# Decoder layer: rotated part of the latent attention's scores in one matmul of full floats in place of three passes of split operands

## The chip, the cores and the metric

One core of one Trainium2 chip. The metric is the device time of one execution in microseconds, median of several runs; lower is better. A core has TensorE (matmuls, weight loads beside them), VectorE (DVE), ScalarE (ACT), GpSimd (POOL) and SyncE (SP), each with its own queue, and DMA engines.

## What is computed

One decoder layer over 512 tokens of width 2048: modulation, a combined input projection, two attentions (A with a sparse selection of keys, B with latent keys and values), gates, an output projection and a convolutional feed-forward part. The change concerns attention B: 8 heads, whose queries and keys have 128 plain dimensions and 64 rotated ones.

```python
mq = (rms_norm(mq_lat, g_mq_lat) @ w_mq_up).reshape(B, S, M_HEADS, M_NOPE + M_ROPE)
mkv = (rms_norm(mkv_lat, g_mkv_lat) @ w_mkv_up).reshape(B, S, M_HEADS, M_NOPE + M_V)
...
mk = rms_norm(jnp.concatenate([mk_nope, mk_r], axis=-1), g_km)
mq = rms_norm(mq, g_qm)
mq = jnp.concatenate([mq[..., :M_NOPE], apply_rope(mq[..., M_NOPE:], *rope_m)], axis=-1)
mk = jnp.concatenate([mk[..., :M_NOPE], apply_rope(mk[..., M_NOPE:], *rope_m)], axis=-1)
...
logits = jnp.einsum('bthd,bshd->bhts', q_b, k, preferred_element_type=jnp.float32) * scale
logits = jnp.where(causal[None, None], logits, -jnp.inf)
p = jax.nn.softmax(logits, axis=-1).astype(v.dtype)
return jnp.einsum('bhts,bshd->bthd', p, v).reshape(B, Q_BLOCK, H * dv)
```

The scores of a head are thus a sum of a product over 128 dimensions and one over 64.

## The kernel before, in words

Activations and weights lie in SBUF in tiles of 128 rows and 512 columns ("slots", 81 of them, handed out by `get` and given back by `put`). Results of matmuls go to eight banks of PSUM. Two kinds of matmul are used. The projections split each operand into a high part of type float32r and a low part, the rest (`split`: a copy on ScalarE, line 138, and a subtraction on VectorE, line 139; `wtile` does the same for weights, lines 130 and 131) and run three passes: high by high, high by low, low by high (lines 142 to 144). Some products in the attentions run as one matmul of plain float32; in the trace such a matmul is two records.

Work goes in stages: modulation and input projection; attention A with gates; the remaining gates by a scheme of seven products (line 1072 on); then attention B with the projection of A's output; the projection of B's output (`w_pb`); the output projection (`w_o`); the feed-forward part.

In the attention B stage, `up_pair(hp)` projects queries, keys and values of two heads from the latents (`lin_tm`), normalizes and rotates them in `ev_up` and `ev_qup`, and transposes them (lines 1165, 1169, 1200, 1204) so that the dimension lies on the rows. The plain parts get a tile per head (`kT[a]`, `qT[a]`); the rotated parts of both heads share one, head `a` in rows 64a to 64a+63, which is split (lines 1170 and 1205) into `kTr` and `qTr`. `attend_pair(hp)` then takes both heads through `attend`: for each of four blocks of 128 queries, the longest first, the scores `qk` go into a bank, with S = 512, 384, 256, 128 keys. A score block is four matmuls:

```python
W = max(S, 256)
PE.matmul(o[:, :W], qh[rs, qs], kh[rs, :W], start=True, stop=False)
PE.matmul(o[:, :W], qh[rs, qs], kl[rs, :W], start=False, stop=False)
PE.matmul(o[:, :S], qT[a][:, qs], kT[a][:, :S], start=False, stop=False)
PE.matmul(o[:, :W], ql[rs, qs], kh[rs, :W], start=False, stop=True)
```

Three of them (lines 1219, 1220, 1222) have 64 rows, since `rs` is half of the rows; the third (line 1221) has 128 rows and plain floats. Behind a block comes the softmax on VectorE and ScalarE (lines 689 to 692), behind four blocks the transposes of the probabilities (line 700) and the product with the values (line 708, plain floats), whose result is split (lines 710 and 711) and, but for the last two heads, stored to DRAM.

`pa_block` (the projection of A's output, three passes) stands between the pairs of heads, and a background stream multiplies modulation weights on VectorE (line 747). The order on each engine isn't that of the source: a scheduler orders instructions by priorities and its own estimate of times, so score blocks stand between matmuls of projections. Weight loads of SP go ahead at high priority (`wtile`), as buffers come free.

Of the kernel before, what the change touches and what calls it, by code (L numbers as in the profile page):

```python
# [14 lines left out]
AF = mybir.ActivationFunctionType  # L15
# [16 lines left out]
def trunk_layer_kernel(  # L32
# [21 lines left out]
    V, A, G, PE, SP = nc.vector, nc.scalar, nc.gpsimd, nc.tensor, nc.sync  # L54
# [14 lines left out]
    def get(dt=F32):  # L69

        i = min(free, key=lambda n: rested[n])
        free.remove(i)
        if cur[i] is None or cur[i].dtype != dt:
            cur[i] = pool.tile([P, T], dt, name=f"slot{i}", tag=f"slot{i}")
        held[id(cur[i])] = i
        return cur[i]

    def getr():
        return get(F32R)

    def put(*ts, lag=2):

        for t in ts:
            i = held.pop(id(t))
            rested[i] = clock[0] + lag
            free.append(i)
# [26 lines left out]
    def r32(ap):  # L113
        return ap.bitcast(F32)
# [22 lines left out]
    def split(dst_hi, dst_lo, src):  # L137
        A.activation(dst_hi, src, AF.Copy)  # L138
        V.tensor_tensor(dst_lo, src, r32(dst_hi), ALU.subtract)  # L139
# [103 lines left out]
    def rsqrt_mean(dst, ss, n, w):  # L243
        v = sm.tile([P, w], F32, name="rsm")
        V.tensor_scalar(v, ss, 1.0 / n, EPS, op0=ALU.mult, op1=ALU.add)
        G.tensor_tensor(dst, v, mhalf[:, :w], ALU.pow)
# [271 lines left out]
    def at_bank():  # L518
        cnt["at"] += 1
        return AT[cnt["at"] % 4]  # L520
# [6 lines left out]
    b = bank[7]  # L527
# [10 lines left out]
    b = bank[6]  # L538
# [7 lines left out]
    for tb in range(1, 4):  # L546
        S = (tb + 1) * P
        qiT = []
        for cb in range(2):
            t = qi[tb, cb]  # L550
            rope(t.rearrange("p (h d) -> p h d", d=64), 8, 16, "i", tb)
            b = at_bank()
            for q in range(4):
                PE.transpose(b[:, q * P:(q + 1) * P], t[:, q * P:(q + 1) * P], ident)
            o = (getr(), getr())
# [5 lines left out]
        for hd in range(16):  # L561
            ps = slice((hd % 2) * 64, (hd % 2) * 64 + 64)
            q = (hd % 8) // 2
            b = at_bank()
# [40 lines left out]
    def head_ss(dst, src3, i):  # L605
        n, d = src3.shape[1], src3.shape[2]
        t = sq[i % 2][:, :n * d].rearrange("p (n d) -> p n d", n=n)
        A.activation(t, src3, AF.Square)
        V.tensor_reduce(dst, t, axis=AX.X, op=ALU.add)
# [16 lines left out]
    for g in range(2):  # L626
        b = at_bank()
# [46 lines left out]
    def attend(*a):  # L674
        attend_pv(*attend_p(*a))
# [251 lines left out]
    def operands(act, ts):  # L927
        return (quarter(act, 0, 0), quarter(act, KH, 0), quarter(act, KH, HT)) + tuple(sums(ts, n) for n in range(4))
# [14 lines left out]
    def seven(work, pairs_of_banks, hook=None, AHEAD=2):  # L943
        def pair_steps(n, p):
            bx, by = pairs_of_banks[n % len(pairs_of_banks)]
            X, Y, Z = bx[:, :HT], by[:, :HT], by[:, HT:]
            L, E = {}, {}
            W = p.K * P
            g1, g2 = p.scale or (None, None)
# [5 lines left out]
            def load(blk):  # L955
                t = rawq.popleft()
                SP.dma_start(t[:, :W], p.load(blk))
                return t

            def hilo(t):  # L960
                i = cnt["wt"] % len(hi_b)
                cnt["wt"] += 1
                hi, lo = hi_b[i][:, :W], lo_b[i][:, :W]
                split(hi, lo, t[:, :W])
                return hi, lo

            def comb(o, a, b, op):
                V.tensor_tensor(o[:, :W], a[:, :W], b[:, :W], op)  # L968

# [116 lines left out]
    for i in range(KH // 2):  # L1086
        raw = [get() for _ in range(4)]
        ta, tb_ = get(), get()
        for j in range(2):
            k, o = 2 * i + j, slice(j * HT, (j + 1) * HT)  # L1090
# [10 lines left out]
    def gate_out(i):  # L1101
        def fin(u1, u2):
            G.dma_start(gate_d[G0 + 2 * i], u1)
            G.dma_start(gate_d[G0 + 2 * i + 1], u2)
            put(u1, u2)
        return fin
# [10 lines left out]
    def gate_hook(q, n):  # L1117
        gate_tick()
        if q == n - 7:
            reload_mq()  # L1120

    rs = operands(h, h_sums)
    start, run = seven([Pair(rs, lambda blk, i=i: w_gs[i, blk], gate_out(i)) for i in range((31 - G0) // 2)],
          ((MM[0], MM[1]), (MM[2], MM[3])), gate_hook)
# [10 lines left out]
    def up_pair(hp):  # L1135
        kn = [get() for _ in range(2)]
        vv = [get() for _ in range(2)]
        kr = get()
        kr3 = kr.rearrange("p (t a d) -> p t a d", t=4, a=2)

        def two(ts, tb):
            o = (tb % 2) * 256
            return ts[tb // 2][:, o:o + 256].rearrange("p (n d) -> p n d", n=2)

        def ev_up(tb, b, kn=kn, vv=vv, kr3=kr3, two=two):
            b4 = b.rearrange("p (n e d) -> p n e d", n=2, e=2)
            k3 = two(kn, tb)
            A.activation(k3, b4[:, :, 0, :], AF.Copy)
            V.tensor_copy(two(vv, tb), b4[:, :, 1, :])
            ss = sm.tile([P, 2], F32, name="ss2")  # L1150
            head_ss(ss, k3, tb)
            V.tensor_scalar(ss, ss, ss_kr[:, tb:tb + 1], None, op0=ALU.add)
            r = sm.tile([P, 2], F32, name="rs2")
            rsqrt_mean(r, ss, 192, 2)
            V.tensor_tensor(k3, k3, r[:, :, None].to_broadcast([P, 2, P]), ALU.mult)
            for a in range(2):
                V.tensor_scalar(kr3[:, tb, a], krot[:, tb], r[:, a:a + 1], None, op0=ALU.mult)

        lin_tm(w_mkv_up, hp * 512, 512, kvT, 2, MM, ev_up)
        kT = [get(), get()]  # L1160
        kTr = (getr(), getr())
        for a in range(2):
            b = at_bank()
            for tb in range(4):
                PE.transpose(b[:, tb * P:(tb + 1) * P], two(kn, tb)[:, a, :], ident)
            A.activation(kT[a], b, AF.Copy, scale=gkm_col)
        b = at_bank()
        for tb in range(4):
            PE.transpose(b[:, tb * P:(tb + 1) * P], kr[:, tb * P:(tb + 1) * P], ident)
        split(*kTr, b)  # L1170
        put(*kn)
        put(kr)

        qn = [get() for _ in range(2)]
        qr = get()
        qr3 = qr.rearrange("p (t a d) -> p t a d", t=4, a=2)
        nsc_b = sm.tile([P, 4, 2], F32, name="nsc_b", bufs=3)

        def ev_qup(tb, b, qn=qn, qr3=qr3, nsc_b=nsc_b, two=two):
            b3 = b.rearrange("p (n d) -> p n d", n=2)  # L1180
            q3 = two(qn, tb)
            A.activation(q3, b3[:, :, 0:P], AF.Copy)
            V.tensor_copy(qr3[:, tb], b3[:, :, P:192])
            ss = sm.tile([P, 2], F32, name="ss2")
            t = sq[tb % 2][:, :384].rearrange("p (n d) -> p n d", n=2)
            A.activation(t[:, :, 0:P], q3, AF.Square)
            A.activation(t[:, :, P:192], qr3[:, tb], AF.Square)
            V.tensor_reduce(ss, t, axis=AX.X, op=ALU.add)
            r = sm.tile([P, 2], F32, name="rs2")
            rsqrt_mean(r, ss, 192, 2)  # L1190
            V.tensor_scalar(nsc_b[:, tb], r, -(192 ** -0.5), None, op0=ALU.mult)
            rope(qr3[:, tb], 2, 64, "qm", tb)

        lin_tm(w_mq_up, hp * 384, 384, mqT, 4, MM, ev_qup)
        qT = [get(), get()]
        qTr = (getr(), getr())
        for a in range(2):
            b = at_bank()
            for tb in range(4):
                PE.transpose(b[:, tb * P:(tb + 1) * P], two(qn, tb)[:, a, :], ident)  # L1200
            A.activation(qT[a], b, AF.Copy, scale=gqm_col)
        b = at_bank()
        for tb in range(4):
            PE.transpose(b[:, tb * P:(tb + 1) * P], qr[:, tb * P:(tb + 1) * P], ident)
        split(*qTr, b)
        put(*qn)
        put(qr)
        pairs[hp] = (qT, qTr, kT, kTr, vv, nsc_b, two)

    def attend_pair(hp):  # L1210
        qT, qTr, kT, kTr, vv, nsc_b, two = pairs.pop(hp)
        for a in range(2):
            rs = slice(a * 64, (a + 1) * 64)

            def qk(o, qb, S, a=a, rs=rs, qT=qT, qTr=qTr, kT=kT, kTr=kTr):
                qs = slice(qb * P, (qb + 1) * P)
                (qh, ql), (kh, kl) = qTr, kTr
                W = max(S, 256)
                PE.matmul(o[:, :W], qh[rs, qs], kh[rs, :W], start=True, stop=False)
                PE.matmul(o[:, :W], qh[rs, qs], kl[rs, :W], start=False, stop=False)  # L1220
                PE.matmul(o[:, :S], qT[a][:, qs], kT[a][:, :S], start=False, stop=False)
                PE.matmul(o[:, :W], ql[rs, qs], kh[rs, :W], start=False, stop=True)

            attend(qk, lambda qb: Z[:, 384 - qb * P:512], lambda qb, a=a, n=nsc_b: n[:, qb, a:a + 1],
                   lambda kc, a=a, vv=vv, two=two: two(vv, kc)[:, a, :], *(ob_d[hp * 2 + a] if hp < 3 else (None, None)))
        put(*vv)
        put(*kT)
        put(*qT)
        put(*kTr, *qTr)


    pa_d = [dram.tile([P, T], F32, name=f"pa{k}") for k in range(KD)]
# [4 lines left out]

    ada_in_slots[0] = False
    up_pair(0)
    oa = reload(oa_d)  # L1240
    up_pair(1)
    attend_bufs()
    for hp in range(4):
        attend_pair(hp)
        pa_block(hp)
        if hp < 2:
            up_pair(hp + 2)
# [273 lines left out]
    rs = operands(h2, tsum)  # L1521
# [108 lines left out]
```

## Time and profile before

| | us |
|---|---|
| median of three runs (2674.61, 2672.03, 2675.9) | 2674.61 |
| profiled execution | 2672.67 |
| its span in the profile | 2670.9 |
| rotated scores, first and last start | 833.9 and 1038.2 |

Views of the profile: the page gives the busy time of each engine; stretches give the same for a window of time, with the granted clock of TensorE (PEclk) and the share of the DMA engines; the order of time gives start, duration, engine, line, operation, written and read tiles, rows and columns; PE is the matmul, PEld the weight load, which runs beside it. In a shape, `64*128 64x512` is 64 rows, 128 columns of weights, and 512 moving columns. Records of one line that follow each other are merged ("x2"). Starts are as recorded, ends of matmuls are modelled, so distances are taken from start to start.

### The profile page before, as it was taken

The numbers are of one execution on the slowest core, as the hardware profiler recorded it, in microseconds if no ns is written. First come the engines' busy times: TensorE is split into PE (matmuls) and PEld (weight loads), VectorE is DVE, ScalarE is ACT, GpSimd is POOL, SyncE is SP. The second block draws the span as 40 slices with busy tenths as digits, with TensorE's granted clock in tenths as the row PEclk, the third lists the DMA queues.
The fourth block names the chain that finished last, engine by engine and source line by source line (L and its number), as shares of the span: only waits on it lengthen the run. The fifth ranks groups of instructions, "written<-read, shape, count | busy, mean of one in ns | idle before, by whom it ended". The sixth has DMA issues, their size and how long they took to land. (4 is left out here: it accounts for less than half of the span.)

```text
span 2670.9 us, 45030 instructions
## 1 busy us (share of the span) xinstructions
PE 2610.9 (98%) x17200; PEld 2351.5 (88%) x17200; DVE 2178.5 (82%) x3499; ACT 1268.3 (47%) x1967; POOL 362.3 (14%) x663
## 2 busy tenths in 40 slices
PE   6999999999999999999999999999999999999999
PEld 6877787778997777788789999999999999999999
DVE  7976976779878676984569989989989889878787
ACT  4333434334445456322445555555555556655454
POOL 1000011010022123110100000000001024423120
PEclk8999899999999999999999999999999999999999
DMA  9943036664675478982323343343334447767563
GB/s 342 340 161 107 28 111 192 214 221 154 197 250 175 136 255 269 319 303 97 140 82 137 119 146 122 120 145 121 128 137 149 129 149 217 211 159 207 143 205 115
DMA packets 215661, 464.31 MB, mean 174 GB/s; under 512 B 23786, under 2 KB 65156, under 8 KB 215444
## 3 DMA queue, kind: packets, MB, share of 16 engines
q1 hardware_dynamic: 170260, 344.93, 39.4%
q0 software_dynamic: 45152, 116.50, 14.9%
q8 instruction: 134, 2.20, 0.3%
q14 instruction: 83, 0.68, 0.1%
q10 hardware_dynamic: 32, 0.01, 0.0%
HBM read 397.11 MB, written 64.23 MB: 173 GB/s over the span
## 5 line engine op out<-in xcount | busy, mean ns | idle before, releaser
L1072 PE MATMUL bank<-slot,whl 128*128 128x256 f32 x3920 | 1104.2, 283 | 20.5 <-ACT slot L972 5.5
L1073 PE MATMUL bank<-slot,whl 128*128 128x256 f32 x3920 | 1099.9, 282 | 0.2 <-DVE slot L139 0.2
L1074 PE MATMUL bank<-slot,whl 128*128 128x256 f32 x3920 | 1088.0, 281 | 6.3 <-DVE whl L139 6.3
L138 ACT ACTIVATE whl<-raw 128x1024 fp32r<-128x1024 f32 (+2 forms) x560 | 532.7, 953 | 617.2 <-PE bank L1073 404.3
L1072 PEld LDWEIGHTS bank<-slot,whl 128*128 128x128 f32 x3920 | 739.6, 189 | 27.7 <-ACT slot L972 8.2
L1073 PEld LDWEIGHTS bank<-slot,whl 128*128 128x128 f32 x3920 | 740.8, 189 | 0.6 <-DVE slot L139 0.5
L1074 PEld LDWEIGHTS bank<-slot,whl 128*128 128x128 f32 x3920 | 733.4, 189 | 7.5 <-DVE whl L139 7.5
L139 DVE TENSOR_TENSOR whl<-raw,whl 128x1024 fp32r<-128x1024 f32 (+2 forms) x560 | 605.7, 1087 | 121.2 <-ACT whl L138 118.9
L130 ACT ACTIVATE whl<-raw 128x1024 fp32r<-128x1024 f32 (+4 forms) x182 | 187.4, 1031 | 383.8 <-PE bank L144 201.9
L968 DVE TENSOR_TENSOR raw<-raw 128x1024 f32<-128x1024 f32 (+2 forms) x320 | 347.1, 1085 | 6.3 <-DMA raw<-in_w_ups 3.4
L131 DVE TENSOR_TENSOR whl<-raw,whl 128x1024 fp32r<-128x1024 f32 (+4 forms) x182 | 215.8, 1187 | 153.4 <-ACT whl L130 152.8
L143 PE MATMUL bank<-whl,slot 128*128 128x512 f32 (+2 forms) x768 | 297.1, 388 | 0.0
L142 PE MATMUL bank<-whl,slot 128*128 128x512 f32 (+2 forms) x768 | 290.3, 391 | 3.2 <-ACT slot L409 3.2
L144 PE MATMUL bank<-whl,slot 128*128 128x512 f32 (+2 forms) x768 | 292.9, 385 | 0.0
L142 PE MATMUL bank<-slot,whl 128*128 128x512 f32 (+1 forms) x656 | 261.7, 403 | 3.1 <-ACT slot L1358 2.3
L143 PE MATMUL bank<-slot,whl 128*128 128x512 f32 (+1 forms) x656 | 262.5, 400 | 1.4 <-DVE slot L711 1.3
L144 PE MATMUL bank<-slot,whl 128*128 128x512 f32 (+1 forms) x656 | 257.4, 401 | 0.4 <-DVE whl L131 0.4
L142 PEld LDWEIGHTS bank<-whl,slot 128*128 128x128 f32 x768 | 146.1, 190 | 33.4 <-ACT slot L409 3.3
L747 DVE SCALAR_TENSOR_TENSOR slot<-slot,c_act,slot 128x512 f32<-128x512 f32 x203 | 149.0, 746 | 32.4 <-DMA slot<-in_w_ada 31.1
L143 PEld LDWEIGHTS bank<-whl,slot 128*128 128x128 f32 x768 | 146.2, 190 | 28.9 <-issue 0.5
L144 PEld LDWEIGHTS bank<-whl,slot 128*128 128x128 f32 x768 | 144.7, 189 | 29.5 <-issue 0.5
L142 PEld LDWEIGHTS bank<-slot,whl 128*128 128x128 f32 (+1 forms) x656 | 122.5, 187 | 33.6 <-issue 2.8
(290 smaller groups left out, 2763.9 us busy)
## 6 DMA issues: line engine op xcount, KB each, us to landing
slot<-in_w_ada SPq DMA_DIRECT2D x344, 256.0 KB, 5.7
raw<-in_w_ups SPq DMA_DIRECT2D x160, 512.0 KB, 4.9
raw<-in_w_in SPq DMA_DIRECT2D x50, 512.0 KB, 3.4
raw<-in_w_down SPq DMA_DIRECT2D x64, 384.0 KB, 4.1
raw<-in_w_down SPq DMA_DIRECT2D x64, 320.0 KB, 3.5
slot<-f POOLq DMA_DIRECT2D x154, 128.0 KB, 3.7
f<-slot POOLq DMA_DIRECT2D x66, 256.0 KB, 5.2
raw<-in_w_gs SPq DMA_DIRECT2D x32, 512.0 KB, 4.4
```

Source lines behind the costliest of these rows:

```text
L130: A.activation(hi, raw[:, :w], AF.Copy)
L131: V.tensor_tensor(lo, raw[:, :w], r32(hi), ALU.subtract)
L138: A.activation(dst_hi, src, AF.Copy)
L139: V.tensor_tensor(dst_lo, src, r32(dst_hi), ALU.subtract)
L142: PE.matmul(o, lh, rh, start=first, stop=False)
L143: PE.matmul(o, lh, rl, start=False, stop=False)
L144: PE.matmul(o, ll, rh, start=False, stop=last)
L747: V.scalar_tensor_tensor(acc, ts[i], c_act[:, k:k + 1], acc, op0=ALU.mult, op1=ALU.add)
L968: V.tensor_tensor(o[:, :W], a[:, :W], b[:, :W], op)
L1072: PE.matmul(o, wh[:, ks], rh, start=first and k == 0, stop=False, skip_group_check=True)
L1073: PE.matmul(o, wh[:, ks], rl, start=False, stop=False, skip_group_check=True)
L1074: PE.matmul(o, wl[:, ks], rh, start=False, stop=last, skip_group_check=True)
```

## The change

The rotated parts are no longer split. One slot each of plain floats takes the place of the high and low parts, written by the copy on ScalarE that wrote the high part. The scores take one 64-row matmul of plain floats over S columns (no longer at least 256), ahead of the 128-row one. In the new kernel these are lines 1217 and 1218.

```diff
-        kTr = (getr(), getr())
+        kTr = get()
...
-        split(*kTr, b)
+        A.activation(kTr, b, AF.Copy)
...
-        qTr = (getr(), getr())
+        qTr = get()
...
-        split(*qTr, b)
+        A.activation(qTr, b, AF.Copy)
...
-                (qh, ql), (kh, kl) = qTr, kTr
-                W = max(S, 256)
-                PE.matmul(o[:, :W], qh[rs, qs], kh[rs, :W], start=True, stop=False)
-                PE.matmul(o[:, :W], qh[rs, qs], kl[rs, :W], start=False, stop=False)
-                PE.matmul(o[:, :S], qT[a][:, qs], kT[a][:, :S], start=False, stop=False)
-                PE.matmul(o[:, :W], ql[rs, qs], kh[rs, :W], start=False, stop=True)
+                PE.matmul(o[:, :S], qTr[rs, qs], kTr[rs, :S], start=True, stop=False)
+                PE.matmul(o[:, :S], qT[a][:, qs], kT[a][:, :S], start=False, stop=True)
...
-        put(*kTr, *qTr)
+        put(kTr, qTr)
```

## Prediction

> **What bounds the kernel now.** I read the page first, for the share of each engine.
>
> ```profile
> span 2670.9 us, 45030 instructions
> ...
> PE 2610.9 (98%) x17200; PEld 2351.5 (88%) x17200; DVE 2178.5 (82%) x3499; ACT 1268.3 (47%) x1967; POOL 362.3 (14%) x663
> ```
>
> TensorE is busy all the time, but an average of the span says nothing of one stage. The rotated scores (lines 1219, 1220, 1222) run from 834 to 1039 us, so I asked for the stretches around them.
>
> ```profile
> core 0: us, PE busy (x) PEld busy (x) DVE busy (x) ACT busy (x) POOL busy (x), PEclk, DMA share, GB/s
> 790.00:1040.00 250.00, 250.00 (x1134) 186.45 (x1133) 180.07 (x508) 135.98 (x261) 70.36 (x113) 1.00 0.65 208
> 1040.00:1060.00 20.00, 19.59 (x84) 14.60 (x82) 9.44 (x18) 11.06 (x17) 7.30 (x14) 1.00 0.92 338
> 1060.00:1200.00 140.00, 137.87 (x593) 111.11 (x593) 130.59 (x190) 48.45 (x65) 17.50 (x31) 1.00 0.88 305
> ```
>
> From 790 to 1040 us TensorE has no idle time at all, at full clock (PEclk 1.00), while VectorE works 180 of 250 us and ScalarE 136. Nothing feeds TensorE late there, so each nanosecond that its stream of instructions gets shorter shortens the span. The stage behind it (1060 to 1200) is also TensorE's (137.87 of 140), with VectorE close behind (130.59).
>
> "Busy" is not "at its peak", though: ends of matmuls are modelled. The waits of that stretch (us in total, times, longest) name the weight loads of just these lines, with "issue", i.e. no other engine, as what ended them.
>
> ```profile
> PEld bank L1222 <- issue: 12.2, 24, 0.8
> ...
> PEld bank L1221 <- issue: 5.2, 17, 0.4
> ...
> PEld bank L1219 <- issue: 4.7, 14, 0.4
> ```
>
> So I read TensorE's order of time and took distances from start to start, not durations.
>
> ```profile
> 859.01 0.39 PE L144 MATMUL bank<-whl,slot 128*128 128x512 f32 x1
> 859.33 0.44 PE L1219 MATMUL bank<-slot,slot 64*128 64x384 f32 x1
> 859.61 0.33 PE L1220 MATMUL bank<-slot,slot 64*128 64x384 f32 x1
> 859.87 0.91 PE L1221 MATMUL bank<-slot,slot 128*128 128x384 f32 x2
> 860.71 0.44 PE L1222 MATMUL bank<-slot,slot 64*128 64x384 f32 x1
> 860.99 0.28 PE L1219 MATMUL bank<-slot,slot 64*128 64x256 f32 x1
> 861.11 0.28 PE L1220 MATMUL bank<-slot,slot 64*128 64x256 f32 x1
> 861.31 0.70 PE L1221 MATMUL bank<-slot,slot 128*128 128x256 f32 x2
> 861.94 0.38 PE L1222 MATMUL bank<-slot,slot 64*128 64x256 f32 x1
> 862.25 0.50 PE L142 MATMUL bank<-whl,slot 128*128 128x512 f32 x1
> 862.59 0.40 PE L143 MATMUL bank<-whl,slot 128*128 128x512 f32 x1
> ...
> 869.29 0.34 PE L142 MATMUL bank<-whl,slot 128*128 128x384 f32 x1
> 869.47 0.34 PE L143 MATMUL bank<-whl,slot 128*128 128x384 f32 x1
> ```
>
> Two score blocks stand here, of 384 and of 256 keys. What does each pass take when nothing is in its way? A split pass of 256 columns takes 0.12 us (860.99 to 861.11, both 64 rows), one of 384 takes 0.18 (869.29 to 869.47), one of 512 takes 0.23 (836.88 to 837.11 below). A matmul of full floats is two records ("x2"), and its price is that of the probability-times-value matmuls, line 708, which are of the same kind:
>
> ```profile
> 836.88 0.39 PE L144 MATMUL bank<-slot,whl 128*128 128x512 f32 x1
> ...
> 837.11 0.40 PE L142 MATMUL bank<-slot,whl 128*128 128x512 f32 x1
> ```
> ```profile
> 865.13 1.46 PE L708 MATMUL bank<-slot,slot 128*128 128x384 f32 x6
> 866.52 0.49 PE L1219 MATMUL bank<-slot,slot 64*128 64x512 f32 x1
> ...
> 868.67 0.44 PE L142 MATMUL bank<-whl,slot 128*128 128x384 f32 x1
> 868.95 0.34 PE L143 MATMUL bank<-whl,slot 128*128 128x384 f32 x1
> ```
>
> Six records are matmuls of 384, 256 and 128 columns: 768 columns in 1.39 us, of which I put about 0.1 to the visible half of the following switch, so 1.29 us or 1.68 ns a column (a split pass: 0.45).
>
> Now the two blocks above. The stream before them ends at 859.01 + 0.23 = 859.24; L143 starts at 862.59, so L142 streamed from 862.36. Between lie 3.12 us. The passes need 3 x 0.18 + 3 x 0.12 for the split ones and 640 columns x 1.68 ns = 1.08 for the full ones: 1.98 us. **The other 1.14 us are gaps**, and each stands where a 64-row matmul meets a 128-row one: 1219 after 144, 1221 after 1220, 1222 after 1221, and again, and 142 after 1222: six changes (between 1222 and the next 1219 there is none), 0.19 us each. The block of 512 keys at 866.52 gives the same: 866.42 to 868.77 is 2.35 us, passes 3 x 0.23 + 0.86 = 1.55, four changes, 0.20 each. It is the length of one weight load of these lines, seen in full:
>
> ```profile
> L1219 PEld LDWEIGHTS bank<-slot,slot x32: 182/183/187, 833.9 to 1038.2; 64*128 64x128 f32 x32
> ```
>
> **The change part by part.**
>
> *Fewer changes of height.* A score block was 64, 64, 128, 64 rows high; it becomes 64, 128. Alone, a block then has two changes in place of four. Counted over the instruction order of the two built programs, TensorE changes between 64 and 128 rows 118 times in this stage before and 62 times after. 56 x 0.19 = **-10.6 us**, on the path since TensorE has no idle time.
>
> *Other passes.* Per head (blocks of 512, 384, 256 and 128 keys; the split passes of the last ran 256 wide) three split passes take 3 x (0.23 + 0.18 + 0.12 + 0.12) = 1.95 us. The full-float one has 1280 columns: 1280 x 1.68 ns = 2.15 us. That is +0.2 x 8 heads = **+1.6 us**. The trace has no 64-row matmul of full floats. From above its price is bounded by twice that of the 128-row one (half of the rows streamed at half the rate), +17.2 us; from below by half (its two records side by side in the two halves of the array), -8.6 us. I take the 128-row price, since rows of both heights agree for the split passes: 0.12 us for 256 columns.
>
> [...] By passes alone the kernel would get slower by the 1.6 us. [...]
>
> *The split of both rotated operands.* ScalarE's copy stays (it writes plain floats in place of rounded ones); VectorE's subtraction goes, for four pairs and two operands:
>
> ```profile
> L139 DVE TENSOR_TENSOR slot<-bank,slot 128x512 fp32r<-128x512 f32 x8 | 5.5, 686 | 4.8 <-ACT slot L138 4.7
> ```
>
> 5.5 us of VectorE, which is busy 180 of 250 us here and which TensorE does not wait for: 0. Were that cover gone it would be a further gain, not a cost. Two slots fewer are held per operand pair; nothing in TensorE's row waited for a slot, so 0 again.
>
> *What moves.* The scheduler writes another order: in TensorE's list some 940 of 17,000 instructions stand elsewhere, nearly all in this stage and the projection behind it; SP's list moves 20 DMA issues, none with new bytes. Most of it is matmuls of one weight tile before those of another, and costs 0 while operands are early. One place I can price, the first use of the last heads' output:
>
> ```profile
> 1053.74 2.32 PE L708 MATMUL bank<-slot,slot 128*128 128x512 f32 x8
> ...
> 1058.86 1.20 PE L142 MATMUL bank<-slot,whl 128*128 128x512 f32 x4
> 1061.41 0.50 PE L143 MATMUL bank<-slot,whl 128*128 128x512 f32 x1 [1.35 <-DVE slot L711]
> ```
>
> TensorE stands still for 1.35 us until VectorE has the low half. In the new order this L143 stands 6.5 us of matmuls behind the last L708 (3.7 before, same prices), 2.8 us more, so the wait should go: **-1.4 us**. Bounds: -1.4, and as much the other way if another wait of this length appears; behind it 1060 to 1200 is bound by the same engine, and no wait is late next.
>
> **Sum:** -10.6 + 1.6 - 1.4 = -10.4 us. The profiled execution took 2672.67 us (its span 2670.9 and 1.8 around it); it would take 2662.3. The median of three is 2674.61, 1.9 above it, so I forecast **2664.2 us** for the median.
>
> **The rivals.**
>
> 1. *The second weight load shows too.* A full-float matmul loads weights twice. For 128 rows the second load hides (1.68 ns a column holds over six records); if at 64 rows it doesn't, each of 32 blocks has a third gap: 32 x 0.19 = 6.1, leaving -4.3: 2670.3. Against it: 1219 to 1220 in 0.12 us, a 64-row load hidden behind a 64-row pass.
> 2. *The gaps stay.* If they belong to a score block and not to the change of height, the passes alone decide: +1.6, 2676.2. Against it: the block at 860.99 has no gap of 0.19 on its first side, where a 64-row matmul precedes.
> 3. *Slower: half the array at half the rate.* The mechanism is in TensorE, line 1217 of the new kernel: if 64 rows of full floats stream at 3.4 ns a column, the scores pay 8 x 2.15 = 17.2 more, +6.8: 2681.4. It decides from a price 1.6 times that of the 128-row matmul (10.4 of 17.2). For it: no row shows this kind. Against it: height makes no difference to split passes.
> 4. *The gain is given back in the next stage.* From 1060 to 1200 VectorE has 9.4 us to spare and the transfers run at 305 GB/s; if the projection there has to wait for either until the old time, nothing is left: 2674.6. Against it: that stage only starts earlier, it doesn't get shorter, and its transfers are issued as buffers come free, so they move along.
> 5. *Cheaper than thought:* the two halves at once, -10.4 - 8.6: 2655.6.
>
> That the change doesn't do what it says is out: the built program has 64 TensorE instructions fewer.
>
> **How the numbers follow.** Forecast 0.72; rival 1 0.09; rival 2 0.04; rival 3 0.05; rival 4 0.06; rival 5 0.04. The measurement can tell about 0.2%, 5.3 us, from no change. Forecast and rival 5 are faster by more: 0.76. Rivals 1, 2 and 4 lie within: 0.19. Rival 3 is slower: 0.05. The forecast's own band is some 4 us to each side: the three runs before spread over 3.9 us, a wait of 1.4 may stay or another appear, and 0.01 us in the price of a change is 0.6. The range 2659.5 to 2671.0 holds that band and rival 1, 0.81; the bounds of the unknown price (rivals 3 and 5) lie outside with 0.09.
>
> **What would show it.** The row to compare with is that of the 128-row records:
>
> ```profile
> L1221 PE MATMUL bank<-slot,slot 128*128 128x512 f32 x16 | 9.0, 645 | 0.0
> ```
>
> In the new profile: score blocks of 64 rows x2 and then 128 rows x2, with about 0.19 us more than passes at the start of each of the two and none before the following split pass; 64-row records as long as the 128-row ones of their width (the row above); about 10 us less between the start of the first score and the end of the last; no L143 waiting for line 711; 790 to 1030 still without idle time. A block of 512 keys that takes over 2.2 us (passes 2 x 0.86, changes 2 x 0.19: 2.1) makes it wrong (rivals 1 to 3), and so does a next stage whose TensorE row shows several us of new idle time (rival 4).

## The result, and the profile after

The changed kernel takes 2679.68 us (median of 20 runs, 2673.27 to 2688.16), the kernel before in its runs beside them 2675.78 (20 runs, 2672.03 to 2677.65). The ratio is 1.0017, 95% interval 1.0009 to 1.0024: slower by 4 us, where 10.4 us less were forecast. The profiled execution took 2681.41 us, 8.7 more than that of before. The runs after also scatter over 15 us, those before over 6. Where times of different runs are compared below, they are given as ratios to runs of the kernel before on the same chip, which moved from chip to chip by 3 us.

First the scores, in TensorE's order of time after the change: two score blocks of 256 and 128 keys (lines 1217 and 1218).

```profile
848.29 0.40 PE L143 MATMUL bank<-slot,whl 128*128 128x512 f32 x1
848.62 0.70 PE L1217 MATMUL bank<-slot,slot 64*128 64x256 f32 x2
849.24 0.70 PE L1218 MATMUL bank<-slot,slot 128*128 128x256 f32 x2
849.87 0.48 PE L1217 MATMUL bank<-slot,slot 64*128 64x128 f32 x2
850.29 0.49 PE L1218 MATMUL bank<-slot,slot 128*128 128x128 f32 x2
850.53 0.48 PE L144 MATMUL bank<-slot,whl 128*128 128x512 f32 x1
850.85 0.39 PE L142 MATMUL bank<-slot,whl 128*128 128x512 f32 x1
```

From 848.52 (848.29 + 0.23) to 850.62 (850.85 - 0.23) are 2.10 us. The passes, at 1.68 ns a column, need 768 x 1.68 = 1.29; the other 0.81 are four changes of height, 0.20 each. After the last L1218 there is no gap. The groups by shape of the same stretch show the unknown of the prediction, the 64-row matmul of full floats, as dear as the 128-row one (635 and 638 ns a record of 512 columns):

```profile
L1218 PE MATMUL bank<-slot,slot 128*128 128x512 f32 x16 | 8.9, 638 | 0.0
...
L1217 PE MATMUL bank<-slot,slot 64*128 64x512 f32 x16 | 8.9, 635 | 0.0
```

So the passes and the changes of height cost what was forecast. The prediction's other signs failed: from the start of the first score to that of the last matmul of a score are 199.7 us for 205.2, not some 10 less, TensorE is idle for 4.1 of the 250 us from 790 to 1040, and an L143 still waits for line 711. To see where the gain went I cut the execution at two places that every version has: the last matmul of the gates stage (791 us before) and the first transpose of the residual (line 1323 before, 1304 us). The stretch between holds attention B and both projections behind it. Before and after, with the rest of the span:

```profile
791.10:1304.30 513.20, 510.66 (x2247) 395.21 (x2246) 361.08 (x761) 221.73 (x381) 94.62 (x155) 1.00 0.65 217
1304.30:2670.90 1366.60, 1341.55 (x10875) 1316.52 (x10873) 1188.66 (x1519) 736.55 (x1077) 199.02 (x337) 1.00 0.48 148
```
```profile
791.30:1307.10 515.80, 505.19 (x2215) 391.18 (x2214) 357.57 (x753) 219.83 (x381) 97.05 (x157) 1.00 0.66 216
1307.10:2679.60 1372.50, 1344.28 (x10875) 1318.55 (x10873) 1189.00 (x1519) 736.49 (x1077) 199.33 (x337) 1.00 0.49 147
```

The first number is the length, the second TensorE's busy time. TensorE works 5.5 us less, and the stretch is 2.6 us longer: its idle time went from 2.5 to 10.6 us. Behind the stretch, where nothing was changed, another 5.9 us were lost. TensorE's waits in that stretch (us in total, times, longest), before and then the three longest after:

```profile
PE bank L143 <- DVE slot L711: 1.3, 1, 1.3
PE bank L142 <- DVE slot L790: 0.8, 1, 0.8
PE bank L144 <- DVE whl L131: 0.4, 1, 0.4
```
```profile
PE bank L142 <- DVE slot L790: 4.8, 2, 4.4
PE bank L700 <- DVE slot L692: 2.3, 2, 2.1
PE bank L143 <- DVE slot L711: 1.8, 1, 1.8
```

The longest, by the order of time of TensorE and VectorE:

```profile
1109.58 2.33 DVE L747 SCALAR_TENSOR_TENSOR slot<-slot,c_act,slot 128x512 f32<-128x512 f32 x3
...
1110.50 0.40 PE L783 MATMUL bank<-slot,ones_r 128*128 128x512 f32 x1
1113.90 0.75 DVE L747 SCALAR_TENSOR_TENSOR slot<-slot,c_act,slot 128x512 f32<-128x512 f32 x1 [2.00 <-DMA slot<-in_w_ada]
1114.58 0.68 DVE L790 TENSOR_TENSOR slot<-bank,ident 128x512 f32<-128x512 f32 x1
...
1115.32 0.50 PE L142 MATMUL bank<-slot,whl 128*128 128x512 f32 x1 [4.41 <-DVE slot L790]
```

The flush sums a finished block of the background stream into a bank (line 783 on TensorE) and reads it out (line 790 on VectorE); TensorE's next matmul writes that bank. Line 790 stands in VectorE's queue behind four multiplications of the stream (line 747), and the last of these waits 2.00 us for its own transfer. In the order before, line 790 stood ahead of that last one, behind 190 multiplications of the stream where it now stands behind 191, and it was line 790 that waited for TensorE:

```profile
1110.16 1.64 DVE L747 SCALAR_TENSOR_TENSOR slot<-slot,c_act,slot 128x512 f32<-128x512 f32 x2
1113.24 0.69 DVE L790 TENSOR_TENSOR slot<-bank,ident 128x512 f32<-128x512 f32 x1 [1.44 <-PE bank L783]
```

The wait for line 711, which I had expected to go, has the same form: four L747, the first of them 4.50 us late for a transfer, stand ahead of it. Before, a multiplication that was 3.31 us late stood there too.

```profile
1055.06 3.12 DVE L747 SCALAR_TENSOR_TENSOR slot<-slot,c_act,slot 128x512 f32<-128x512 f32 x4 [4.50 <-DMA slot<-in_w_ada]
1058.10 0.68 DVE L711 TENSOR_TENSOR slot<-bank,slot 128x512 fp32r<-128x512 f32 x1
```

The wait for line 692 comes from ScalarE, which turns between the softmax's exponentials (690) and sigmoids of the gates (1266, 1267), and loads a table at each turn, 1.28 us each. There are 19 such loads in the stretch before and after; before, no matmul waited for line 692.

```profile
1024.18 1.28 ACT L1267 ACT_TABLE_LOAD   x1
...
1026.12 1.28 ACT L690 ACT_TABLE_LOAD   x1
1027.42 0.51 ACT L690 ACTIVATE slot<-slot,mn 128x256 f32<-128x256 f32 x1
...
1028.66 0.55 PE L700 MATMUL bank<-ident,slot 128*128 128x128 f32 x3 [2.06 <-DVE slot L692]
```

Last, the clock. Stretches of 3.4 us around two waits, after the change; PEclk is the third column from the end:

```profile
1112.60:1116.00 3.40, 0.69 (x3) 0.60 (x4) 2.10 (x4) 0.00 (x0) 0.00 (x0) 0.99 0.97 337
1116.00:1119.40 3.40, 3.40 (x10) 2.62 (x9) 3.40 (x7) 1.06 (x1) 1.61 (x4) 0.50 0.80 246
...
1317.40:1320.80 3.40, 1.37 (x5) 0.85 (x6) 3.37 (x7) 1.97 (x4) 2.32 (x5) 0.99 1.02 392
1320.80:1324.20 3.40, 3.40 (x9) 2.62 (x10) 3.40 (x7) 1.44 (x2) 0.00 (x0) 0.50 0.70 274
```

After a stretch in which TensorE worked 0.69 or 1.37 of 3.4 us, the next one ran at half clock (PEclk 0.50). That 1.7 us are lost each time, half of 3.4, is an estimate; a split pass of 512 columns took 0.43 us there (1116.22 to 1116.65) for 0.23, by which it is 1.6. Before, the same wait of 2.3 us ahead of the feed-forward part fell across two stretches, and the clock stayed (PEclk 1.00):

```profile
1312.10:1315.50 3.40, 2.17 (x19) 1.84 (x17) 1.16 (x2) 2.51 (x6) 3.40 (x7) 1.00 1.04 418
1315.50:1318.90 3.40, 2.26 (x9) 1.57 (x10) 3.40 (x7) 2.39 (x4) 1.39 (x3) 1.00 1.02 381
```

The half-clock stretches after the change begin at 781.5, 1116.0 and 1320.8 us, 98 and 60 steps of 3.413 us apart. In the traces before and after every stretch of one clock but the last is a whole number of such steps long, the shortest one step: a fixed grid. By the rows above half clock followed windows that held 0.69 and 1.37 us of work.

### The profile page after: what moved, and what is told of

It is laid out like the page before. It is cut to its first block, busy times and chain, and to the rows that moved or that the text cites. A ratio compares the mean times of both kernels' runs of the same rounds, so it can differ in the third digit from the quotient of the medians.

```text
span 2679.6 us, 44954 instructions
## 1 busy us (share of the span) xinstructions
PE 2604.5 (97%) x17168; PEld 2344.1 (87%) x17168; DVE 2175.6 (81%) x3491; ACT 1265.8 (47%) x1967; POOL 364.2 (14%) x663
## 4 chain that ended last, share of the span: by engine, by line
PE 71%; issue 12%; DMA 8%; DVE 6%; POOL 2%; ACT 2%; SPq 0%; POOLq 0%; DVEq 0%; ACTq 0%
PE bank L1072 13%; PE bank L1074 13%; PE bank L1073 13%; PE bank L142 9%; PE bank L143 9%; PE bank L144 9%; DMA slot<-in_w_ada 3%; DMA x<-slot 2%; DVE whl L139 1%; DMA raw<-in_w_ada 1%; DVE slot L747 1%; DVE slot L572 0%; PE bank L708 0%; DVE raw L968 0%; PE bank L1218 0%
## 5 line engine op out<-in xcount | busy, mean ns | idle before, releaser
L143 PE MATMUL bank<-whl,slot 128*128 128x512 f32 (+2 forms) x768 | 297.3, 388 | 0.9 <-DVE whl L131 0.9
L143 PE MATMUL bank<-slot,whl 128*128 128x512 f32 (+1 forms) x656 | 264.0, 403 | 1.8 <-DVE slot L711 1.8
L747 DVE SCALAR_TENSOR_TENSOR slot<-slot,c_act,slot 128x512 f32<-128x512 f32 x203 | 148.6, 747 | 37.2 <-DMA slot<-in_w_ada 35.6
L143 PEld LDWEIGHTS bank<-whl,slot 128*128 128x128 f32 x768 | 146.4, 191 | 29.8 <-DVE whl L131 1.4
```

Of the source, the lines that this page charges most:

```text
L143: PE.matmul(o, lh, rl, start=False, stop=False)
L747: V.scalar_tensor_tensor(acc, ts[i], c_act[:, k:k + 1], acc, op0=ALU.mult, op1=ALU.add)
```

## The experiments

**Theory A:** the scores are cheaper as worked out; the new written order puts what TensorE needs behind queue neighbours on VectorE and ScalarE that wait for transfers, and long waits cost half-clock stretches besides (with these, A2). **Theory B:** the written order alone costs the time, or the block itself is slow. **Theory C:** the stages behind are paced by their transfers, so any gain in the scores is given back.

For every profiled execution: length T of the stretch between the two places, TensorE's idle time in it (T less its busy time), the loss by half clock (1.7 us for each 3.4 us stretch, the estimate above), and the rest, which is the price of TensorE's own stream. The cuts are at the exact starts and the entries rounded, so they differ by up to 0.1 from the views above.

| kernel | ratio to before (95%) | T | idle | half clock | rest | against before |
|---|---|---|---|---|---|---|
| before | 1 | 513.3 | 2.5 | 0 | 510.7 | |
| after | 1.0017 (1.0009-1.0024) | 515.8 | 10.6 | 1.7 | 503.5 | -7.2 |
| after, once more | one run | 516.8 | 10.0 | 3.4 | 503.3 | -7.4 |
| adjacent | 0.9979 (0.9971-0.9987) | 510.9 | 8.2 | 1.7 | 500.9 | -9.8 |
| before, no loads | 1.0015 (1.0006-1.0024) | 514.2 | 3.3 | 1.7 | 509.2 | -1.5 |
| after, no loads | 0.9985 (0.9975-0.9994) | 507.5 | 3.7 | 1.7 | 502.1 | -8.6 |
| after, flush first | 0.9996 (0.9987-1.0005) | 511.3 | 6.5 | 1.7 | 503.1 | -7.6 |
| tall | 0.9950 (0.9937-0.9964) | 502.1 | 8.3 | 1.7 | 492.1 | -18.7 |
| adjacent, flush first | 0.9976 (0.9964-0.9987) | 501.4 | 1.0 | 0 | 500.4 | -10.3 |
| tall, flush first | 0.9984 (0.9975-0.9993) | 506.7 | 10.3 | 6.8 | 489.6 | -21.1 |
| after, queues | 1.0001 (0.9993-1.0010) | 510.6 | 5.8 | 3.4 | 501.4 | -9.3 |
| tall, queues | 0.9952 (0.9939-0.9966) | 498.5 | 6.1 | 1.7 | 490.7 | -20.0 |
| after, warm | 1.0003 (0.9995-1.0012) | 515.5 | 9.1 | 3.4 | 503.0 | -7.7 |
| after, swapped | 0.9998 (0.9989-1.0007) | 507.7 | 4.7 | 0 | 503.0 | -7.8 |

**The changed kernel once more.**

> The changed kernel once more, for a second profile. Theory A (VectorE works its queue in order, and a multiplication of the background stream that waits for a late transfer of w_ada holds what TensorE needs): the scores take the same time as in the first profile to 0.3 us, but the waits behind them (for the low half of the last outputs, line 711, and for the flush, line 790) differ by over 1 us, as the transfers come at other times. Theory B (the written order alone costs the time): the same waits within 0.5 us.

2683.36 us in one run. TensorE's price is the same to 0.2 us, but from the first score to the last are 202.1 us for 199.7, since a wait now lies between them, against the expectation. The waits: line 790 4.5 us in two waits (4.8 before), line 711 0.7 (1.8), a new wait of 2.0 for line 705, and five half-clock stretches of 3.4 us behind the gates stage where the first profile has two. The same program doesn't meet the same waits, as A says; for line 711 they differ by over 1 us, but for 790 they agree to 0.3 us, as B says.

**Three split passes next to one another.**

```diff
-PE.matmul(o[:, :S], qT[a][:, qs], kT[a][:, :S], start=False, stop=False)
-PE.matmul(o[:, :W], ql[rs, qs], kh[rs, :W], start=False, stop=True)
+PE.matmul(o[:, :W], ql[rs, qs], kh[rs, :W], start=False, stop=False)
+PE.matmul(o[:, :S], qT[a][:, qs], kT[a][:, :S], start=False, stop=True)
```

> The kernel before with its three split 64-row passes next to one another and the 128-row one last: two changes of height per block in place of four, no other pass, the split kept. Both theories: the scores get some 10.6 us shorter (56 changes by 0.19). Theory A: most of it is given back behind the scores where VectorE's queue waits for w_ada: 0 to 6 us faster than before. Theory B: anything between 10 us faster and 5 us slower, with waits at other places than lines 711 and 790.

2668.55 us, 5 us faster than before. Its instruction order has 70 changes of height for 118: 48 x 0.19 = 9.1, and the rest fell by 9.8. This is the change's gain without the change: no pass, no split was touched. Half was given back again, 4.3 us of it at line 790, where a multiplication waited 3.06 us for its transfer.

**The stream without its transfers, before and after.**

```diff
-                if ada_in_slots[0]:
+                if fixed:
+                    ts = fixed
+                elif ada_in_slots[0]:
...
+                if fixed:
+                    pass
+                elif ada_in_slots[0]:
...
+    fixed.extend([get(), get()])
+    for i in range(2):
+        SP.dma_start(fixed[i], w_ada[i * P:(i + 1) * P, 4096:4608])
     up_pair(0)
...
+    put(*fixed)
```

> The kernel before, with the background stream from the attention B stage on multiplying two tiles that lie in SBUF already, in place of transfers of w_ada (so these modulation columns are computed from the wrong blocks; every instruction on VectorE stays). Theory A: the waits of TensorE for lines 711 and 790 shrink from 1.35 and 0.8 us to under 0.3 together; 2 to 4 us faster than before. Theory B: no change beyond 2 us.

> The changed kernel with the same stream without transfers (the same columns wrong). Theory A: without late transfers nothing holds VectorE's queue, the gain of the scores stays: 6 to 10 us faster than the kernel before without transfers. Theory B: still slower than, or equal to, the kernel before without transfers (0 to +5 us).

In runs side by side 2677.72 and 2668.96 us: the changed kernel is faster by 8.8 us, where with transfers it was slower by 4. Its idle time fell from 10.6 to 3.7 us, as A says and against C. The other half missed: the kernel before got slower by 4 us without the transfers, not faster by 2 to 4. Its waits for lines 711 and 790 did shrink, from 2.1 to 0.5 us, but two of 2.3 us together for line 692 came. Its profile has three half-clock stretches (at 938, 1317 and 2232 us) where the kernel before has none, and another order. So the pair shows the gain, and not that transfers alone held it.

**The flush ahead of the stream.**

```diff
-                V.tensor_tensor(a3, b.rearrange("p (q n) -> p q n", q=4),
-                                ident[:, None, :].to_broadcast([P, 4, P]), ALU.mult)
+                flushed[0] = V.tensor_tensor(a3, b.rearrange("p (q n) -> p q n", q=4),
+                                             ident[:, None, :].to_broadcast([P, 4, P]), ALU.mult)
...
-                        V.scalar_tensor_tensor(acc, ts[i], c_act[:, k:k + 1], acc,
-                                               op0=ALU.mult, op1=ALU.add)
+                        with tc.issue_after(flushed[0].ins) if flushed[0] else nullcontext():
+                            V.scalar_tensor_tensor(acc, ts[i], c_act[:, k:k + 1], acc,
+                                                   op0=ALU.mult, op1=ALU.add)
```

> The changed kernel, with the multiplications of the background stream ordered behind the flush (line 790) that the projection's bank waits for, where the changed kernel has four of them, one with a late transfer, ahead of it. Theory A2 (queue order on VectorE with a late transfer, and TensorE's clock halved for 3.4 us after the long wait): the wait of 4.4 us for line 790 falls below 1 us, no halved clock at about 1115 us, -3.6 - 1.7: 2674.5 in all. Theory C (the stage is paced by its transfers, whatever the order): the wait moves to a later place, time unchanged within 1.5 us of the changed kernel.

2672.59 us, ratio 0.9996 for 1.0017: 0.21% or 5.6 us gained against the changed kernel, as A2 says (5.3), and against C. Part of the agreement is luck: the half clock in the stretch is as long as without the edit (1.7 us), at another place. The wait for line 790 and the half clock at 1116 us are gone from the profile:

```profile
PE bank L142 <- ACT slot L710: 2.7, 1, 2.7
PE bank L1219 <- DVE slot L703: 1.4, 1, 1.4
PE bank L700 <- DVE slot L692: 1.4, 2, 1.1
```

Others stand in their place (line 710, the copy of the last output, with a half-clock stretch behind it).

**Full height.**

```diff
-        qTr = get()
+        qTr = [get(), get()]
...
-        A.activation(qTr, b, AF.Copy)
+        for a in range(2):
+            G.memset(qTr[a][(1 - a) * 64:(2 - a) * 64], 0.0)
+            A.activation(qTr[a][a * 64:(a + 1) * 64], b[a * 64:(a + 1) * 64], AF.Copy)
...
-                PE.matmul(o[:, :S], qTr[rs, qs], kTr[rs, :S], start=True, stop=False)
+                PE.matmul(o[:, :S], qTr[a][:, qs], kTr[:, :S], start=True, stop=False)
...
-        put(kTr, qTr)
+        put(kTr, *qTr)
```

> The changed kernel, with the rotated queries of each head in a tile of their own whose other 64 rows are zero, so that the full-float matmul is 128 rows high over both heads' keys: no change of height at all (0 in the instruction order, 62 in the changed kernel). The price of a change of height, 0.19 us, gives -11.8 us in the scores. Theory A2: of that 3 to 6 are given back behind the scores; 2668 to 2674. Theory C: all is given back, as transfers pace the stage: 2677 to 2681.

2659.25 us (5 runs), ratio 0.9950 (0.9937 to 0.9964): faster than both kernels, by more than A2 allowed. No change of height is left; 118 x 0.19 - 1.6 = 20.8 us against before were expected, the rest fell by 18.7. In its order of time the blocks of 256 and 128 keys stand without gaps:

```profile
845.29 0.39 PE L143 MATMUL bank<-slot,whl 128*128 128x512 f32 x1
845.52 0.59 PE L1219 MATMUL bank<-slot,slot 128*128 128x256 f32 x2
845.95 0.59 PE L1220 MATMUL bank<-slot,slot 128*128 128x256 f32 x2
846.38 0.38 PE L1219 MATMUL bank<-slot,slot 128*128 128x128 f32 x2
846.60 0.39 PE L1220 MATMUL bank<-slot,slot 128*128 128x128 f32 x2
```

From 845.52 to 846.38 are 0.86 us for two matmuls of 256 columns: 512 x 1.68 ns. Twice the rows, half of them zeros, cost TensorE nothing here: a column still takes 1.68 ns.

**Adjacent passes and full height, with the flush ahead of the stream.** The edits are those above together.

> Three split passes next to one another (70 changes of height in place of 118 without the flush ordered, 68 with it), and the stream ordered behind the flush as in the run with that name. Theory A2: as fast as the run with adjacent passes alone or up to 4 us faster, 2664 to 2669. Theory C: no faster than that run, 2668 to 2670.

> Both: full height and the stream ordered behind the flush. Theory A2: most of 11.8 + 3.6 + 1.7 against the changed kernel stays: 2662 to 2668. Theory C: 2677 to 2681.

The first: 2665.71 us, ratio 0.9976 for 0.9979, in range, with 1.0 us idle and no half clock in the stretch. The second missed: 2669.72, slower than full height alone by 10 us (ratio 0.9984 for 0.9950). Its price is the lowest of all (-21.1), but it has 10.3 us of waits and loses 6.8 to half clock. The longest wait, in the order of time of ScalarE and TensorE:

```profile
1050.05 0.63 ACT L1271 ACTIVATE slot<-slot 128x512 f32<-128x512 f32 x1 [2.66 <-DMA slot<-gate]
...
1051.67 0.63 ACT L1270 ACTIVATE slot<-slot 128x512 f32<-128x512 f32 x1 [0.99 <-DMA slot<-gate]
...
1052.21 0.58 ACT L710 ACTIVATE slot<-bank 128x512 fp32r<-128x512 f32 x1
...
1052.84 1.65 PE L142 MATMUL bank<-slot,whl 128*128 128x512 f32 x3 [4.38 <-ACT slot L710]
```

Here sigmoids that wait for gate transfers stand ahead of line 710. Moving one queue neighbour moved the others.

**Three groups moved at once.** To the edit of the flush come these; the sigmoids stand behind the last copy on ScalarE, their products and the stream behind the last low half on VectorE.

```diff
+        ends[0] = A.activation(oh, ob, AF.Copy)
+        ends[1] = V.tensor_tensor(ol, ob, r32(oh), ALU.subtract)
...
+    flushed[0] = ends[1]
...
+            with tc.issue_after(ends[0].ins):
+                A.activation(g, g, AF.Sigmoid)
+                A.activation(b, b, AF.Sigmoid)
+            with tc.issue_after(ends[1].ins):
+                V.tensor_tensor(a, a, g, ALU.mult)
```

> The changed kernel with three groups moved behind what TensorE waits for: the gates' sigmoids on ScalarE behind the copy of the last output's high part, their multiplications on VectorE behind its low part, and the background stream behind that and behind each flush. Theory A2 (the gain of 9 us is there, and is lost to such queue neighbours and to the halved clock after long waits): TensorE's waits between the gates stage and the transposes of the residual fall from 10 to 3 us, about as before (2.5); 2664 to 2669. Theory C (the stage is paced by its transfers): waits of 6 us or more remain; 2672 to 2680.

> The full-height version with the same three groups moved. Theory A2: 21 us less in price than before, waits of about 3 us: 2654 to 2659, and less spread than the full-height version alone. Theory C: 2660 or more.

Both missed: 2672.68 (ratio 1.0001) and 2662.06 (0.9952, as full height alone), and the scatter of the second is 10 us for 6, not less. Both times lie in the ranges that theory C gave, though the first's waits (5.8 us) are just under its 6. ScalarE's table loads in the stretch fall from 19 to 1 and its work by some 23 us, which TensorE doesn't gain. In the first, the three waits are smaller or gone, and a new one of 2.9 us came at the flush for the split on ScalarE (line 138), with two half-clock stretches (3.4 us lost) behind it:

```profile
PE bank L785 <- ACT slot L138: 2.9, 1, 2.9
...
PE bank L143 <- DVE slot L711: 1.2, 1, 1.2
PE bank L142 <- ACT whl L130: 1.0, 1, 1.0
```

**TensorE kept at work in a wait.**

```diff
+            bc[0] = PE.matmul(b[:, tb * P:(tb + 1) * P], cols[:, tb:tb + 1].to_broadcast([P, P]), ident,
+                              start=True, stop=True)
...
     x1_T(3, half())
+    with tc.issue_after(bc[0].ins):
+        for _ in range(20):
+            PE.transpose(bk[0][:, 0:P], ident, ident)
```

> The changed kernel with 20 transposes of the identity, 2.2 us, which nobody reads, in TensorE's wait of 2.5 us ahead of the feed-forward part; the rest of the order as it is. If the halved clock of 3.4 us at about 1320 us comes of the idle wait: it is gone, -1.7 us in the executions that had it, 0 to 2.5 us faster than the changed kernel in the median. If it comes of something else (the load, the clock's own time): it is there still, no change.

2672.28 us, ratio 1.0003 for 1.0017: 3.7 us faster than the changed kernel, more than expected. Up to these 20 instructions TensorE's order is that of the changed kernel; right behind them some hundred matmuls stand in another order, and on VectorE some 40 to 50 instructions moved, so not all of the 3.7 need be the clock's. At the place itself the half clock is gone:

```profile
1310.30:1313.70 3.40, 2.96 (x26) 2.45 (x24) 0.96 (x4) 3.40 (x9) 2.95 (x6) 1.00 1.00 385
1313.70:1317.10 3.40, 3.26 (x29) 3.02 (x29) 2.45 (x5) 2.20 (x5) 2.98 (x6) 1.00 1.03 402
1317.10:1320.50 3.40, 3.36 (x14) 2.45 (x14) 3.40 (x6) 2.11 (x4) 0.54 (x1) 1.00 0.99 382
```

**The same block in the other order, 128 rows first.**

```diff
-                PE.matmul(o[:, :S], qTr[rs, qs], kTr[rs, :S], start=True, stop=False)
-                PE.matmul(o[:, :S], qT[a][:, qs], kT[a][:, :S], start=False, stop=True)
+                PE.matmul(o[:, :S], qT[a][:, qs], kT[a][:, :S], start=True, stop=False)
+                PE.matmul(o[:, :S], qTr[rs, qs], kTr[rs, :S], start=False, stop=True)
```

> The changed kernel with the two matmuls of a score block in the other order (128 rows first): the same passes and changes of height, another written order everywhere behind. Theory A2: the price between the gates stage and the residual's transposes is the same within 1.5 us, and the waits differ from the changed kernel's by 2 us or more in either direction; 2667 to 2681. A theory by which the two-matmul block as such is slow: the same time within 1.5 us.

2672.67 us, ratio 0.9998: 5 us faster than the changed kernel with the same work. Its price is the same (-7.8 and -7.2), its idle time 4.7 us for 10.6. This is what rules out that the block as such is slow. Line 790 stands in the same place of VectorE's queue as in the changed kernel, behind 191 multiplications, but the transfer ahead of it was 0.60 us late for 2.00, and TensorE waited 1.4 us for 4.4.

## Why the prediction was wrong

**What bounds the kernel** was right as far as it went: TensorE had no idle time from 790 to 1040 us. But that was a property of one written order, not of the stage: of fourteen profiles of this stretch only one has less idle time than before (1.0 against 2.5 us).

**Fewer changes of height (-10.6) and other passes (+1.6)** held: together -9.0, measured -7.2 to -9.3 in the seven profiles with the two-matmul block and transfers or without, and -9.8 and -18.7 to -21.1 where 48 and all 118 changes went. In the changed kernel's own profile 1.8 of the 9.0 are missing; no run shows where. The 64-row price was that of the 128-row matmul (635 and 638 ns a record of 512 columns); its bounds, twice and half of that, were my estimates, and no run shows either. Rivals 1, 2, 3 and 5 are out.

**What failed is the step "What moves":** that another order "costs 0 while operands are early", with -1.4 for the one place that I priced. That place kept its wait (1.75 us), because I counted TensorE's matmuls between producer and reader and not what stands ahead of line 711 in VectorE's own queue, and whether that waits for a transfer. With the new order as a whole came 8.1 us more of idle time and 1.7 of half clock in the stretch: -7.2 + 8.1 + 1.7 = +2.6, the measured difference. The half clock was no term of the sum. Rival 4 named the place, the next stage, and VectorE's short supply of time there. I gave it 0.06, since its transfers "move along", and let the range hold one wait of 1.4 us. Spare time over a stage says nothing of who stands first in a queue.

**The 5.9 us behind the stretch** had no term at all. Half clock at 1320.8, behind the wait ahead of the feed-forward part, makes 1.7 of it; ten of the fourteen profiles have such a stretch there, so the profile before may have been lucky to have none. A wait of 1.4 us for line 139 at 1434 us, which the kernel before doesn't have, is another part. The remaining 2.8 us, most of it in the feed-forward part, stay open: the order there is nearly the same, and half-clock stretches and waits come and go between executions (two and five such stretches in the changed kernel's two profiles).

That all gains are given back, as C has it, falls by the flush, the full-height and the swapped runs; that a part is, stands. B's slow block falls by the last. Three profiles with the changed kernel's order on TensorE (the first, the second, and that with the transposes) have T from 515.5 to 516.8 us, so its loss comes back with the order. How much of the idle time is the order's alone and how much the late transfers' isn't separated: every edit wrote another order, and the order before with the new block was not tried. The long wait for line 790 took both, a multiplication ahead of it and a late transfer: it is gone with the flush first, and 1.4 us in the swapped order, whose transfer was less late.

## What to carry to other kernels

Where TensorE switches between matmuls of different height inside a stream, look for the gap from start to start (here 0.19 to 0.20 us a change), and group matmuls of one height or pad them to full height before changing their type: here padding with zeros took all of the gaps, the price fell by 18.7 us, and a column still took 1.68 ns. In a kernel whose order is written by a scheduler, a local gain of 10 us has to be weighed against reshuffled queues: read the queue ahead of each instruction that the critical engine waits for, on its own engine, and give the range the spread that several equal orders have (here 5 us between two orders of the same work). In this kernel waits of 4.4 and 2.3 us that left TensorE 0.69 and 1.37 us of work in a window of 3.4 us cost it twice, since half clock followed; before, one of 2.3 us across two windows did not.

## What the runs showed of the hardware that I had not expected

In the profiles before and after the half clock came in whole steps of 3.413 us (the last, at the end of the span, apart), on a grid that doesn't start with the wait: the one for line 790 ended at 1115.3, the half clock began at 1116.0. One and the same wait of 2.3 us ahead of the feed-forward part was followed by half clock when 1.37 of a 3.4 us stretch were work, and not when it was cut into stretches with 2.17 and 2.26. Over all fourteen profiles, from 650 us on, each full-clock window of this grid with up to 1.54 us of work by the profile was followed by half clock, and none with 1.95 us or more; between these it went either way. On the exact grid of the profiles before and after, windows with 0.39, 0.65, 1.00 and 1.33 us were followed by it, one with 1.77 was not. So in these runs where the grid lay decided whether such a wait cost 1.7 us more, by the estimate above. The two profiles of the changed kernel have two and five half-clock stretches behind the gates stage; that this is part of why its runs scatter is likely, but not shown.
